# A two-block network on one core: convolution weights off GpSimd, a three-round inverse in the recurrence, finer modulation pieces

## The chip, the cores and the metric

The kernel runs on one core of a Trainium2 chip, as one program in one launch. The metric is the device time of an execution in microseconds (us), lower is better. The five engines are PE (matrix products), DVE (vector work, most of it elementwise), ACT (functions, copies and casts), POOL (GpSimd) and SP, which here only issues transfers (DMA).

## The reference, cut to what matters

Two blocks follow each other on 512 tokens of width 1024, in fp32. Each has two layers; each layer is a mixer and a feed-forward part, with a modulation (shift, scale, gate) computed from a condition vector by a matrix of its own. The parts that the change touches:

```python
# block 1, second mixer: a gated product, a depthwise convolution of width 31, norm, silu
def _conformer_conv(h, w_in, dw, dw_b, ln_g, ln_b, w_out):
    a, g = jnp.split(h @ w_in, 2, axis=-1)
    z = a * jax.nn.sigmoid(g)
    z = _depthwise_conv(z, dw, dw_b)
    z = jax.nn.silu(_layer_norm(z, ln_g, ln_b))
    return z @ w_out

# block 2, first mixer: a recurrence over time for 8 heads of 64, in both directions
def step(state, inp):
    r_t, w_t, k_t, v_t, kk_t, a_t = inp
    sa = jnp.einsum('bhvk,bhk->bhv', state, -kk_t)
    state = (state * w_t[:, :, None, :] + sa[..., None] * (kk_t * a_t)[:, :, None, :]
             + v_t[..., None] * k_t[:, :, None, :])
    return state, jnp.einsum('bhvk,bhk->bhv', state, r_t)

# ... with a bonus, added to the recurrence's normalised output
bonus = jnp.sum(f['r'][:, :, None] * f['k'] * prm['r_k'], axis=(2, 4))

# block 2, second mixer: one input projection for a neighbourhood and a global attention
p_ctx = u_ctx @ w_in
p_lat = u_lat @ w_in
```

The first mixer of block 2 joins the recurrence with a windowed attention; both run over 512 tokens and 256 context tokens.

## The kernel before, in words

**Products.** An fp32 product of the large weights runs as three products of rounded numbers (`mm3`, L300 to L304): high by high (L302), low by high (L303), high by low (L304). A weight comes by DMA on SP's queue (L285, `wraw_...`), ACT casts it to its high part (L289, `whi_...`), and an engine that is a parameter subtracts to get the low part (L290, `wlo_...`; DVE if nothing is said). L287 multiplies a down weight by a gate before that. hT, the layer's transposed input, is split in the same way (L277 high, L278 low).

**Stages, in us of the profiled execution.** Start 0 to 60; first mixer to 182; first feed-forward to 625; convolution mixer to about 900; second feed-forward to 1345; input products of the recurrence and of the windowed attention (`even`) to 1629; windowed attention, 24 units, to 1753; recurrence to 2117; output product and feed-forward to 2730; input products of the second layer (`odd`) to 2900; its attentions to 3055; the last output product and feed-forward to 3471.

**What sets the order.** A tile scheduler orders each engine's instructions from the code; some places are written out by hand. Modulations are computed in the gaps: `ada_store` puts 512 of a modulation's columns through `ada_part`: four loads of 512 KB (`adaw`, two buffers), 64 matmul records (`adaps`, L209), one ACT copy (`adarows`, L211), and stores. `todo` is a list of such pieces, and each call of `fill()` in a stage pops one.

**Convolution (`mixer1`).** 1024 channels are eight chunks. `gated(f)` makes the two products of a chunk (`cvps`), a sigmoid on ACT, and their gated product on DVE (L603, `hidl`). The 31 taps run as multiply-adds on DVE (L621) for chunks 0 to 4 and most of 7, and as three products with a diagonal matrix (`dg`, made by ACT) on PE for 12 taps of chunk 7 and all of 6 and 5 (`conv_pe`, `cvacc`); for these the chunk is split into zh and zl on DVE (L631, L632, L278) inside `conv_pe`. The projection's low weights wlo_cvin, and those of the first half of the output projection (wraw_dn, wlo_dn), are made on POOL. Behind the last tap PE transposes the chunks (`cvt`), DVE takes statistics (L675), and the result goes through a norm, silu and the output product.

**Even input (`even`).** A list of jobs is run `staggered`: K, Q, U are columns of the projection, W and C decays and rates, G gates, H the attention's heads, B the bonus products (`bops`, L1209) on inputs kd and plt of DVE.

**Recurrence.** Six steps of two chunks, in two directions d. For each, `operators` inverts a block-triangular matrix from the inverses Xd of its 16x16 diagonal blocks: in two doubling levels (16, then 32), V = MM[b] x XT (`pV`, copied by ACT to U), then X plus its product with U (`pX`, added by DVE, L1483), in both transposes at the first level. The result multiplies Aw (`pW`), and that QB (`pD`). In the trace the large buffers are called big, WhThi and WhTchi. The recurrence's first step (`PM`, on AB) begins behind four attention units; Xd comes from an earlier step through DRAM (L1451).

**Odd input (`odd`).** The values are products of six token tiles with four weight pieces (wraw_inv, whi_inv; `dps`), behind eight pieces of queries and keys whose results are stored and loaded again (okh, okl, oq on SP).

Of the kernel before, what the change touches and what calls it, by code (L numbers as in the profile page):

```python
# [21 lines left out]
KD = 8  # L22
# [35 lines left out]
def host_consts():  # L58
# [43 lines left out]
    for b in (16, 32):  # L102
        lv = (t // (2 * b) == u // (2 * b)) & (t % (2 * b) >= b) & (u % (2 * b) < b)
        c4.put(f"lv{b}", np.concatenate([lv & (p[:, None] // 64 == q) for q in range(2)], 1))
# [16 lines left out]
class Kernel:  # L121
# [77 lines left out]
    def ada_part(self, w, sil, c0, bufs=None):  # L199

        nc = self.nc
        acc = self.ps.tile([128, 512], F32, tag="tr", name="adaps", bufs=2)
# [253 lines left out]
    def ffn1(self, li, hT, done, gate, x):  # L456
# [7 lines left out]
        for gi, gn in enumerate(groups):  # L464
            src = []
            for _ in range(gn):
                o = []
                for f in (j, j + NH1):
                    w = self.w_up(wu, 128 * f, "up")
# [8 lines left out]
                self.fill()  # L478
# [10 lines left out]
    def mixer0(self, ws, hT, done, gate, x):  # L489
# [31 lines left out]
        for h in range(4):  # L521
            if h == 2:
                self.fill()
# [19 lines left out]
        for g, win in enumerate(WINDOWS):  # L543
            w = self.w_up(w_in, 1024 + 128 * g, "inz")
# [39 lines left out]
    def mixer1(self, hT, done, gate, x):  # L584
# [8 lines left out]
        def gated(f):  # L593
            self.fill()
# [32 lines left out]
        def conv_pe(f):  # L627
# [10 lines left out]
            nc.vector.tensor_tensor(wl, wf, wh.bitcast(F32), SUB)  # L638
            p = self.mmps("cvacc")
# [9 lines left out]
        order = (0, 1, 2, 3, 4, 7, 6, 5)  # L649
        for j, f in enumerate(order):  # L650
# [28 lines left out]
        conv_pe(5)  # L679
# [29 lines left out]
        with self.tc.issue_after(last.ins):  # L709
            self.down(w_out, src[:4], acc, True, gate=gate, x=x, eng=nc.gpsimd)  # L710
# [4 lines left out]
    def block1(self, xd):  # L715
# [35 lines left out]
        def ada(k, *qs):  # L751
            i, part = phases[k]
            return [lambda q=q: self.ada_store(ap[f"{part}_ada_w"][i], sil, 512 * q, ada1[k]) for q in qs]

        ada2 = [lambda j=j: self.ada_store(ap["w_ada_2"][j // 12], sil2, 512 * (j % 12), self.ada_d[j // 12])
                for j in range(24)]

        def columns():
# [7 lines left out]
                ada(1, 4, 5) + ["gate"] + ada(2, 0, 1, 2, 3) + ["mod"] + ada(2, 4, 5) + ada(3, 0, 1, 2, 3, 4, 5) + ada2[:6],  # L766
                ["gate"] + ["mod"] + ada2[6:12],
                ["gate"] + ada2[12:] + self.begin2()]
# [278 lines left out]
    def even(self, hT):  # L1047
# [200 lines left out]
        jobs += [W[0][3], H[2], B[2], C[0][3], H[3], W[1][3], C[1][3], H[4], H[5], B[3]]  # L1248
# [97 lines left out]
    def recurrence(self, st, R):  # L1346
# [107 lines left out]
        def operators(d, E):  # L1454


            Xd, Aw, QB, AD = (E[x] for x in ("Xd", "Aw", "QB", "AD"))
            X, XT = (v8(bufs[x][d]) for x in ("X", "XT"))
            for x, t in ((1, XT), (0, X)):
# [3 lines left out]
            MM = {}  # L1463
            for b, t in zip((16, 32), bufs["MM"][d]):
                MM[b] = v8(t)
                (nc.gpsimd if E["s"] else vec).tensor_tensor(t.rearrange("p (h q c) -> p h q c", h=8, q=2), E["M"][:, :, None, :].to_broadcast([128, 8, 2, 64]),
                                        c[f"lv{b}"].rearrange("p (q c) -> p q c", q=2)[:, None].to_broadcast([128, 8, 2, 64]), MUL)
# [8 lines left out]
            for b in (16, 32):  # L1476
# [83 lines left out]
        bufs = dict(Aw=at(10, 12, 2, 5), QB=at(11, 13, 7, 6), AD=at(16, 17, 18, 19, 4, 9, 22, 23), X=at(14, 0), XT=at(15, 1),  # L1560
# [378 lines left out]
```

## Time and profile before

| | |
|---|---|
| Median of 3 runs | 3477.03 us |
| All runs | 3480.14, 3477.03, 3469.45 us |
| Profiled execution: own time, span | 3472.81, 3471.0 us |
| Granted clock of PE, mean | 0.959 |
| Busy share: PE, DVE, ACT, POOL | 93%, 59%, 38%, 11% |

The page describes one execution. An engine's busy time is the time in which it works on something; the granted clock is the share of full speed (2.4 GHz, the other level being 1.2 GHz) that PE was given. In a row of the timeline the figure in brackets is the idle time before the instruction, and behind the arrow stands what ended it.

### The profile page before, as it was taken

How to read it: one execution, taken by the hardware profiler on the slowest of the kernel's cores; microseconds unless marked ns; L12 is line 12 of the kernel's file. 1: busy time of each engine (PE TensorE's matmuls, PEld its weight loads, DVE VectorE, ACT ScalarE, POOL GpSimd, SP SyncE). 2: the span in 40 equal slices, each digit the busy share in tenths (PEclk: the TensorE clock that was granted, in tenths of full speed). 3: DMA queues.
4: the chain of work that ended last, by engine and by line, in shares of the span. 5: the costliest groups of instructions: out<-in, count | busy, mean ns of one | idle time of the engine just before them, and what ended most of it. 6: DMA issues, size and time to landing. Idle time of an engine off the chain costs nothing. (4 is left out here: it accounts for less than half of the span.)

```text
span 3471.0 us, 50354 instructions
## 1 busy us (share of the span) xinstructions
PE 3216.5 (93%) x20031; PEld 2612.9 (75%) x20031; DVE 2053.2 (59%) x3772; ACT 1305.7 (38%) x2150; POOL 397.2 (11%) x218
## 2 busy tenths in 40 slices
PE   8989999868999998987898799999999998999998
PEld 5677777746776776875688798788888787878887
DVE  4675554897755567586767667533333735763445
ACT  3243332317423334443543334422222525753222
POOL 0020000540200000023033331010000200010001
PEclk9999999989999998998989899999999999999999
DMA  7645565440266432445322215672222365143332
GB/s 253 202 134 178 175 212 177 133 161 25 86 195 206 125 105 96 124 122 164 90 67 66 64 53 171 142 152 79 65 63 67 122 155 216 63 138 104 97 97 85
DMA packets 520693, 436.67 MB, mean 126 GB/s; under 512 B 91924, under 2 KB 450042, under 8 KB 518922
## 3 DMA queue, kind: packets, MB, share of 16 engines
q1 hardware_dynamic: 520458, 433.45, 41.4%
q8 instruction: 158, 2.59, 0.3%
q14 instruction: 77, 0.63, 0.1%
HBM read 368.96 MB, written 63.78 MB: 125 GB/s over the span
## 5 line engine op out<-in xcount | busy, mean ns | idle before, releaser
L302 PE MATMUL dnps<-whi_dn,hidh 128*128 128x512 f32 x1120 | 442.0, 395 | 3.5 <-ACT hidh L277 2.0
L303 PE MATMUL dnps<-wlo_dn,hidh 128*128 128x512 f32 x1120 | 438.9, 392 | 0.3
L304 PE MATMUL dnps<-whi_dn,hidl 128*128 128x512 f32 x1120 | 435.4, 391 | 1.2 <-DVE hidl L278 1.2
L290 DVE TENSOR_TENSOR wlo_dn<-wraw_dn,whi_dn 128x1024 fp32r<-128x1024 f32 x136 | 167.2, 1230 | 239.1 <-ACT whi_dn L289 238.3
L302 PE MATMUL upps<-hThi,whi_up 128*128 128x512 f32 (+1 forms) x768 | 295.7, 387 | 6.8 <-DVE hThi L277 6.7
L303 PE MATMUL upps<-hTlo,whi_up 128*128 128x512 f32 (+1 forms) x768 | 293.0, 383 | 4.8 <-DVE hTlo L278 4.8
L304 PE MATMUL upps<-hThi,wlo_up 128*128 128x512 f32 (+1 forms) x768 | 290.3, 379 | 0.0
L424 DVE TENSOR_TENSOR acc<-dnps,acc 128x512 f32<-128x512 f32 x200 | 136.7, 687 | 201.7 <-PE dnps L304 201.2
L302 PEld LDWEIGHTS dnps<-whi_dn,hidh 128*128 128x128 f32 x1120 | 210.2, 188 | 60.9 <-ACT hidh L277 7.0
L289 ACT CAST whi_dn<-wraw_dn 128x1024 fp32r<-128x1024 f32 x140 | 147.1, 1051 | 273.7 <-PE dnps L304 101.5
L303 PEld LDWEIGHTS dnps<-wlo_dn,hidh 128*128 128x128 f32 x1120 | 210.5, 188 | 47.1 <-issue 2.7
L304 PEld LDWEIGHTS dnps<-whi_dn,hidl 128*128 128x128 f32 x1120 | 209.8, 188 | 46.7 <-DVE hidl L278 3.4
L303 PE MATMUL up2ps<-hTlo,whi_ff 128*128 128x512 f32 (+1 forms) x576 | 214.5, 373 | 3.4 <-DVE hTlo L278 3.0
L302 PE MATMUL up2ps<-hThi,whi_ff 128*128 128x512 f32 (+1 forms) x576 | 212.7, 371 | 2.4 <-DVE hThi L277 2.4
L304 PE MATMUL up2ps<-hThi,wlo_ff 128*128 128x512 f32 (+1 forms) x576 | 212.1, 369 | 0.0
L290 DVE TENSOR_TENSOR wlo_up<-wraw_up,whi_up 128x1024 fp32r<-128x1024 f32 x88 | 111.1, 1262 | 135.5 <-ACT whi_up L289 134.6
L302 PEld LDWEIGHTS upps<-hThi,whi_up 128*128 128x128 f32 x768 | 147.2, 192 | 54.1 <-issue 12.4
L824 POOL TENSOR_TENSOR ag<-acc,gg 128x1024 f32<-128x1024 f32 x20 | 49.2, 2458 | 1124.8 <-DVE acc L424 1093.5
L303 PEld LDWEIGHTS upps<-hTlo,whi_up 128*128 128x128 f32 x768 | 147.5, 192 | 39.1 <-issue 9.9
L304 PEld LDWEIGHTS upps<-hThi,wlo_up 128*128 128x128 f32 x768 | 147.8, 193 | 26.1 <-issue 0.8
L289 ACT CAST whi_ff<-wraw_ff 128x1024 fp32r<-128x1024 f32 x64 | 67.2, 1052 | 245.9 <-PE dnps L304 202.3
L290 DVE TENSOR_TENSOR wlo_ff<-wraw_ff,whi_ff 128x1024 fp32r<-128x1024 f32 x64 | 80.8, 1264 | 126.7 <-ACT whi_ff L289 126.4
(528 smaller groups left out, 7431.0 us busy)
## 6 DMA issues: line engine op xcount, KB each, us to landing
adaw<-in_w_ada_dram SPq DMA_DIRECT2D x96, 512.0 KB
wraw_up<-in_ffn_w_up_dram SPq DMA_DIRECT2D x88, 512.0 KB
wraw_ff<-in_w_ff_dram SPq DMA_DIRECT2D x64, 512.0 KB
wraw_dn<-in_w_ff_dram SPq DMA_DIRECT2D x64, 512.0 KB
adaw<-in_ffn_ada_w_dram SPq DMA_DIRECT2D x48, 512.0 KB
wraw_dn<-in_ffn_w_down_dram SPq DMA_DIRECT2D x44, 512.0 KB
adaw<-in_mix_ada_w_dram SPq DMA_DIRECT2D x32, 512.0 KB
ab<-ab SPq DMA_DIRECT2D x32, 384.0 KB
```

The source lines that it names most:

```text
L289: nc.scalar.copy(hi, raw)
L290: (eng or nc.vector).tensor_tensor(lo, raw, hi, SUB)
L302: mm(out, a[0], b[0], start=first, stop=False)
L303: mm(out, a[0], b[1], start=False, stop=False)
L304: mm(out, a[1], b[0], start=False, stop=last)
L424: nc.vector.tensor_tensor(acc[:, t, c], p, acc[:, t, c], ADD)
L824: nc.gpsimd.tensor_tensor(ag, a, gg[:, 0 if t < NT else 1, :], MUL)
```

## The change

There are six edits. One: in the convolution the weights wlo_cvin, wraw_dn and wlo_dn are made by DVE, and a chunk for PE is split (`rounded`) as soon as it is gated. Two: `operators` forms one strictly lower block matrix MM (with all levels at once), NT = MM x XT, and three rounds of "NT x what is there, plus the first"; for direction 0 they run on Aw's product with XT, for direction 1 on XT itself, with `pW` behind. Three: the bonus product B[2] stands behind C[0][3] and H[3] in the list of jobs. Four: the recurrence begins behind eight attention units. Five: the odd values run over weight pieces outside and token tiles inside, three tiles at a time. Six: a modulation piece has 256 columns, issues both its loads first, and there are about twice as many calls of `fill()`.

```diff
     def ada_part(self, w, sil, c0, bufs=None):
...
         n = 512 if bufs else 256
-        for c in range(0, 512, n):
-            for h in range(0, KD, 4):
-                raw = bufs.pop(0) if bufs else self.adap.tile([128, 4, 256], F32, tag="adaw", name="adaw", bufs=self.nadaw)
-                nc.sync.dma_start(raw, w[128 * h:128 * h + 512, c0 + c:c0 + c + n].rearrange("(k p) c -> p k c", p=128))
-                for k in range(4):
-                    nc.tensor.matmul(acc[32 * k:32 * k + 32, c:c + n], sil[:, h + k, :], raw[:, k, :], start=h == 0, stop=h > 0)
-        rows = self.wp.tile([128, 512], F32, tag="adar", name="adarows", bufs=1)
+        acc = self.ps.tile([128, n], F32, tag="tr", name="adaps", bufs=2)
+        raw = []
+        for h in range(0, KD, 4):
+            raw.append(bufs.pop(0) if bufs else self.adap.tile([128, 4, 256], F32, tag="adaw", name="adaw", bufs=self.nadaw))
+            nc.sync.dma_start(raw[-1], w[128 * h:128 * h + 512, c0:c0 + n].rearrange("(k p) c -> p k c", p=128))
+        for h, r in zip(range(0, KD, 4), raw):
+            for k in range(4):
+                nc.tensor.matmul(acc[32 * k:32 * k + 32], sil[:, h + k, :], r[:, k, :], start=h == 0, stop=h > 0)
+        rows = self.wp.tile([128, n], F32, tag="adar", name="adarows", bufs=1)
...
     def ada_store(self, w, sil, c0, dst):
-        rows = self.ada_part(w, sil, c0)
-        for m in range(dst.shape[0]):
-            self.nc.sync.dma_start(dst[m, :, c0:c0 + 512], rows[m::32, :])
+        def piece(c):
+            rows = self.ada_part(w, sil, c)
+            for m in range(dst.shape[0]):
+                self.nc.sync.dma_start(dst[m, :, c:c + 256], rows[m::32, :])
+        return [partial(piece, c) for c in (c0, c0 + 256)]
...
         def gated(f):
-            self.fill()
             pp = []
             for ff in (f, f + KD):
-                w = self.w_up(w_in, 128 * ff, "cvin", nc.gpsimd)
+                self.fill()
+                w = self.w_up(w_in, 128 * ff, "cvin")
...
             gated(f)
+            if f in taps_pe:
+                parts.append((f, *rounded(f)))
             for _ in range(14 if j else 0):
                 next(taps)
             if j >= 6:
-                conv_pe(order[j - 1])
+                conv_pe(*parts.pop(0))
...
-            self.down(w_out, src[:4], acc, True, gate=gate, x=x, eng=nc.gpsimd)
+            self.down(w_out, src[:4], acc, True, gate=gate, x=x)
...
-        jobs += [W[0][3], H[2], B[2], C[0][3], H[3], W[1][3], C[1][3], H[4], H[5], B[3]]
+        jobs += [W[0][3], H[2], C[0][3], H[3], B[2], W[1][3], C[1][3], H[4], H[5], B[3]]
...
-            for b in (16, 32):
-                U = v8(R.tile([128, 1024], F32, tag=f"tD{d}", name="U", bufs=2))
+            NT = v8(R.tile([128, 1024], F32, tag=f"tD{d}", name="NT", bufs=2))
+            for hs in H4:
+                nc.scalar.copy(NT[:, hs], mm4("pV", *((XT, MM) if d else (MM, XT)), hs))
+            if not d:
                 for hs in H4:
-                    nc.scalar.copy(U[:, hs], mm4("pV", MM[b], XT, hs))
-                for tr in ((1, 0) if b == 16 else (1 - d,)):
-                    for hs in H4:
-                        t = (XT if tr else X)[:, hs]
-                        vec.tensor_tensor(t, mm4("pX", *((X, U) if tr else (U, X)), hs), t, ADD)
-            XT = X if d == 1 else XT
-            for hs in H4:
-                nc.scalar.copy(Aw[:, hs], mm4("pW", XT, Aw, hs))
+                    nc.scalar.copy(Y[:, hs], mm4("pW", XT, Aw, hs))
+            first, at, to = (Aw, Aw, Y) if d else (Y, Y, Aw)
+            for _ in range(3):
+                for hs in H4:
+                    vec.tensor_tensor(to[:, hs], mm4("pX", NT, at, hs), first[:, hs], ADD)
+                at = to
+            if d:
+                for hs in H4:
+                    nc.scalar.copy(Aw[:, hs], mm4("pW", X, at, hs))
...
-        for t in range(NT2):
-            p = mps()
-            for k in range(KD):
-                wt = ws[k // 2]
-                self.mm3(p, self.cols_of(hT, k, 128 * t, 128),
-                         (wt[0][:, k % 2, :], wt[1][:, k % 2, :]), k == 0, k == KD - 1)
-            nc.scalar.copy(cv[:, t, :], p)
+        for ts in (range(0, 3), range(3, NT2)):
+            ps = [mps() for t in ts]
+            for a, wt in zip(range(0, KD, 2), ws):
+                for t, p in zip(ts, ps):
+                    for k in (a, a + 1):
+                        self.mm3(p, self.cols_of(hT, k, 128 * t, 128),
+                                 (wt[0][:, k % 2, :], wt[1][:, k % 2, :]), k == 0, k == KD - 1)
+            for t, p in zip(ts, ps):
+                nc.scalar.copy(cv[:, t, :], p)
...
-                for _ in range(4):
+                for _ in range(8):
                     next(windowed)
```

On DVE in the convolution, before, at the splits of chunks 6 and 5: hidl_5062 is the gated product of chunk 5, hidl_5064 that of chunk 6, and the zl row is the split of chunk 6.

```order
L621 SCALAR_TENSOR_TENSOR hidh_5065<-hidl_5066,vec_e,hidh_5065 128x506
L287 TENSOR_TENSOR wraw_dn<-wraw_dn,gate 128x1024
L603 TENSOR_TENSOR hidl_5062<-cvps,sg 128x512
L631 MEMSET zh 128x15
L632 MEMSET zh 128x15
L631 MEMSET zl 128x15
L632 MEMSET zl 128x15
L278 TENSOR_TENSOR zl<-hidl_5064,zh 128x512
```

In the changed kernel, on DVE, from the gated product of chunk 6 (hidl_5174) on:

```order
L605 TENSOR_TENSOR hidl_5174<-cvps,sg 128x512
L633 MEMSET zh 128x15
L634 MEMSET zh 128x15
L633 MEMSET zl 128x15
L634 MEMSET zl 128x15
L623 SCALAR_TENSOR_TENSOR hidh_5167<-hidl_5168,vec_e,hidh_5167 128x511
L280 TENSOR_TENSOR zl<-hidl_5174,zh 128x512
L292 TENSOR_TENSOR wlo_cvin<-wraw_cvin,whi_cvin 128x1024 x2
L623 SCALAR_TENSOR_TENSOR hidh_5165<-hidl_5166,vec_e,hidh_5165 128x510
L623 SCALAR_TENSOR_TENSOR hidh_5167<-hidl_5168,vec_e,hidh_5167 128x510
```

The split of chunk 6 stood behind the gated product of chunk 5; now it stands six rows behind its own, and two wlo_cvin stand behind it. Chunk 7's split has moved in the same way.

On PE in the recurrence, before, the operators of the last step for one direction (a program's fp32 product is one of the counted rows here, and two records in a trace):

```order
L323 MATMUL pV<-big 128x128 x8
L323 MATMUL pX<-U,big 128x128 x8
L323 MATMUL pX<-big,U 128x128 x8
L323 MATMUL pV<-big 128x128 x8
L323 MATMUL pX<-big,U 128x128 x8
L323 MATMUL pW<-big 128x128 x8
L323 MATMUL pD<-big 128x128 x16
```

In the changed kernel, at the same place of PE, for one direction:

```order
L325 MATMUL pV<-big 128x128 x8
L325 MATMUL pX<-big,NT 128x128 x24
L325 MATMUL pW<-big 128x128 x8
L325 MATMUL pD<-big 128x128 x16
L325 MATMUL pz<-Z,big 64x64 x16
```

There is one group of V products in place of two, and the three groups of X products stand one behind the other.

## Rows read from the trace of the kernel before

**Rows 1.** Page, part 1: engine, busy us (share of the span), instructions.
```profile
PE 3216.5 (93%) x20031; PEld 2612.9 (75%) x20031; DVE 2053.2 (59%) x3772; ACT 1305.7 (38%) x2150; POOL 397.2 (11%) x218
```

**Rows 2.** Table by windows: us, busy us (instructions) per engine, PEclk, DMA share, GB/s.
```profile
625.00:700.00 75.00, 63.71 (x399) 52.05 (x398) 65.73 (x105) 27.20 (x37) 41.44 (x17) 0.89 0.46 141
700.00:776.00 76.00, 49.66 (x279) 33.62 (x278) 76.00 (x82) 12.40 (x16) 39.90 (x12) 0.85 0.50 161
776.00:860.00 84.00, 72.07 (x319) 56.86 (x319) 67.72 (x126) 60.96 (x161) 2.39 (x1) 0.95 0.08 26
...
1629.00:1753.00 124.00, 96.46 (x892) 75.42 (x891) 82.87 (x279) 68.11 (x212) 8.67 (x16) 0.90 0.39 111
1753.00:2117.00 364.00, 325.31 (x3947) 300.33 (x3946) 255.37 (x554) 130.73 (x239) 123.79 (x80) 0.91 0.25 71
```

**Rows 3.** Waits, 625 to 870 us: total us, times, longest.
```profile
PE cvacc L302 <- DVE zl L632: 22.8, 2, 19.0
...
PE adaps L209 <- DMA adaw<-in_w_ada_dram: 8.3, 4, 5.8
...
PE cvps L303 <- DVE hTlo L278: 7.3, 4, 3.9
```

**Rows 4.** Timeline of DVE, 770 to 870 us: start, us, instruction, idle before.
```profile
813.61 21.80 DVE L621 SCALAR_TENSOR_TENSOR hidh<-hidl,vec_e,hidh 128x497 f32<-128x497 f32 x28
848.77 0.43 DVE L675 BATCH_NORM_STATS2 cvst<-cvt 128x6 f32<-128x256 f32 x1 [13.36 <-PE cvt L667]
```

**Rows 5.** Groups by line, whole span: busy us, mean ns, idle before.
```profile
L621 DVE SCALAR_TENSOR_TENSOR hidh<-hidl,vec_e,hidh 128x503 f32<-128x503 f32 (+15 forms) x169 | 147.2, 916 | 1.9
...
L290 DVE TENSOR_TENSOR wlo_ine<-wraw_ine,whi_ine 128x1024 fp32r<-128x1024 f32 x21 | 25.6, 1218 | 14.7 <-ACT whi_ine L289 14.7
```

**Rows 6.** Groups by line on POOL, 670 to 836 us.
```profile
L290 POOL TENSOR_TENSOR wlo_cvin<-wraw_cvin,whi_cvin 128x1024 fp32r<-128x1024 f32 x9 | 25.3, 2815 | 31.9 <-ACT whi_cvin L289 28.7 <-PE adaps L209 3.1
```

**Rows 7.** Timeline of DVE, 636 to 655 us, the splits of hT.
```profile
640.90 2.50 DVE L278 TENSOR_TENSOR hTlo<-hTf,hThi 128x256 fp32r<-128x256 f32 x1
...
650.25 0.42 DVE L278 TENSOR_TENSOR hTlo<-hTf,hThi 128x256 fp32r<-128x256 f32 x1
```

**Rows 8.** Groups by line, recurrence, 1753 to 2117 us.
```profile
L323 PE MATMUL pV<-WhThi,WhTchi 128*128 128x128 f32 x192 | 28.7, 296 | 0.0
...
L323 PE MATMUL pV<-big 128*128 128x128 f32 x192 | 26.2, 292 | 0.2 <-DVE big L1483 0.2
...
L1483 DVE TENSOR_TENSOR big<-pX,big 128x512 f32<-128x512 f32 x36 | 24.7, 689 | 20.1 <-PE pX L323 19.9
```

**Rows 9.** Waits of PE, recurrence.
```profile
PE pW L323 <- DVE big L1483: 5.4, 1, 5.4
```

**Rows 10.** Timeline of PE, 1585 to 1595 us.
```profile
1589.11 2.90 PE L1209 MATMUL bops<-kd,consts 128*128 128x512 f32 x4 [11.41 <-DVE plt L1172]
...
1593.57 0.39 PE L303 MATMUL lowps<-spl,lwh 64*128 64x512 f32 x1
1593.80 0.39 PE L304 MATMUL lowps<-sph,lwl 64*128 64x512 f32 x1
```

**Rows 11.** Waits of PE, windowed attention, 1629 to 1753 us.
```profile
PE PM L323 <- DMA AB<-ab: 7.7, 1, 7.7
```

**Rows 12.** Timeline of SP's DMA issues, 1640 to 1790 us.
```profile
1709.10 2.62 SPq L1451 DMA_DIRECT2D Xd<-blkout  x4
```

**Rows 13.** Groups by line, whole span, the modulation matmuls.
```profile
L209 PE MATMUL adaps<-adaw,silc 128*32 128x256 f32 (+1 forms) x704 | 59.4, 427 | 12.6 <-DMA adaw<-in_mix_ada_w_dram 6.7 <-DMA adaw<-in_ffn_ada_w_dram 5.6
...
L209 PE MATMUL adaps<-adaw,sil 128*32 128x256 f32 x768 | 57.0, 393 | 16.2 <-DMA adaw<-in_w_ada_dram 15.3
```

**Rows 14.** Timeline of PE, 2855 to 2872 us.
```profile
2868.99 1.22 PE L302 MATMUL dps<-whi_inv,hThi 128*128 128x512 f32 x2 [8.01 <-ACT whi_inv L289]
```

**Rows 15.** Timeline of SP, 2800 to 2910 us.
```profile
2861.63 0.87 SPq L1032 DMA_DIRECT2D okl<-spl  x1
2862.55 1.88 SPq L285 DMA_DIRECT2D wraw_inv<-in_w_in_odd_dram  x2
```

More of the change, by code (lines that the diff above doesn't have):

```diff
@@ L101, in host_consts @@
     c4.put("dg", t // 16 == u // 16)
-    for b in (16, 32):
-        lv = (t // (2 * b) == u // (2 * b)) & (t % (2 * b) >= b) & (u % (2 * b) < b)
-        c4.put(f"lv{b}", np.concatenate([lv & (p[:, None] // 64 == q) for q in range(2)], 1))
+    c4.put("lo", np.concatenate([(t // 16 > u // 16) & (p[:, None] // 64 == q) for q in range(2)], 1))
     c4.put("dg2", p[:, None] // 16 == p[None] // 16)
@@ L201, in ada_part @@
         nc = self.nc
-        acc = self.ps.tile([128, 512], F32, tag="tr", name="adaps", bufs=2)
         n = 512 if bufs else 256
-        for c in range(0, 512, n):
-            for h in range(0, KD, 4):
-                raw = bufs.pop(0) if bufs else self.adap.tile([128, 4, 256], F32, tag="adaw", name="adaw", bufs=self.nadaw)
-                nc.sync.dma_start(raw, w[128 * h:128 * h + 512, c0 + c:c0 + c + n].rearrange("(k p) c -> p k c", p=128))
-                for k in range(4):
-                    nc.tensor.matmul(acc[32 * k:32 * k + 32, c:c + n], sil[:, h + k, :], raw[:, k, :], start=h == 0, stop=h > 0)
-        rows = self.wp.tile([128, 512], F32, tag="adar", name="adarows", bufs=1)
+        acc = self.ps.tile([128, n], F32, tag="tr", name="adaps", bufs=2)
[7 more added lines that the diff above has]
+        rows = self.wp.tile([128, n], F32, tag="adar", name="adarows", bufs=1)
         nc.scalar.copy(rows, acc)
@@ L521, in mixer0 @@
         for h in range(4):
-            if h == 2:
-                self.fill()
+            self.fill()
             w = self.w_up(w_in, 128 * h, "inu")
@@ L543, in mixer0 @@
         for g, win in enumerate(WINDOWS):
+            self.fill()
             w = self.w_up(w_in, 1024 + 128 * g, "inz")
@@ L593, in gated @@
         def gated(f):
-            self.fill()
             pp = []
             for ff in (f, f + KD):
-                w = self.w_up(w_in, 128 * ff, "cvin", nc.gpsimd)
+                self.fill()
+                w = self.w_up(w_in, 128 * ff, "cvin")
                 p = self.mmps("cvps")
@@ L625, in mixer1, with rounded @@
         taps_pe = {7: range(31 - 12, 31), 6: range(31), 5: range(31)}
-        def conv_pe(f):
+        def rounded(f):
             zh = self.tmp("zh", S + 2 * H, F32R)
@@ L638, in conv_pe @@
             nc.vector.tensor_tensor(wl, wf, wh.bitcast(F32), SUB)
+            return zh, zl, wh, wl
+        def conv_pe(f, zh, zl, wh, wl):
             p = self.mmps("cvacc")
@@ L649, in mixer1 @@
         order = (0, 1, 2, 3, 4, 7, 6, 5)
+        parts = []
         for j, f in enumerate(order):
             gated(f)
+            if f in taps_pe:
+                parts.append((f, *rounded(f)))
             for _ in range(14 if j else 0):
@@ L677, in stats @@
                 nc.scalar.copy(zt, p.rearrange("p (t f c) -> p t f c", t=2, f=2))
-        conv_pe(5)
+        conv_pe(*parts.pop(0))
         assert not self.todo
@@ L752, in ada @@
             i, part = phases[k]
-            return [lambda q=q: self.ada_store(ap[f"{part}_ada_w"][i], sil, 512 * q, ada1[k]) for q in qs]
-        ada2 = [lambda j=j: self.ada_store(ap["w_ada_2"][j // 12], sil2, 512 * (j % 12), self.ada_d[j // 12])
-                for j in range(24)]
+            return [f for q in qs for f in self.ada_store(ap[f"{part}_ada_w"][i], sil, 512 * q, ada1[k])]
+        ada2 = [f for j in range(24) for f in self.ada_store(ap["w_ada_2"][j // 12], sil2, 512 * (j % 12), self.ada_d[j // 12])]
         def columns():
@@ L765, in block1 @@
         todo = [ada(0,4,5)+[columns]+ada(1,0,1)+["gate"]+ada(1,2,3)+["mod"],
-                ada(1, 4, 5) + ["gate"] + ada(2, 0, 1, 2, 3) + ["mod"] + ada(2, 4, 5) + ada(3, 0, 1, 2, 3, 4, 5) + ada2[:6],
-                ["gate"] + ["mod"] + ada2[6:12],
-                ["gate"] + ada2[12:] + self.begin2()]
+                ada(1, 4, 5) + ["gate"] + ada(2, 0, 1, 2, 3) + ["mod"] + ada(2, 4, 5) + ada(3, 0, 1, 2, 3, 4, 5) + ada2[:12],
+                ["gate"] + ["mod"] + ada2[12:24],
+                ["gate"] + ada2[24:] + self.begin2()]
         for k, (i, part) in enumerate(phases):
@@ L1457, in operators @@
             Xd, Aw, QB, AD = (E[x] for x in ("Xd", "Aw", "QB", "AD"))
-            X, XT = (v8(bufs[x][d]) for x in ("X", "XT"))
-            for x, t in ((1, XT), (0, X)):
+            X, XT, Y = v8(bufs["X"]), v8(bufs["XT"][d]), v8(bufs["Y"][d])
+            for x, t in ((1, XT), (0, X))[:1 + d]:
                 nc.gpsimd.tensor_tensor(t.rearrange("p h (b s) -> p h b s", b=8),
@@ L1462, in operators @@
                                         c["dg2"].rearrange("p (b s) -> p b s", b=8)[:, None].to_broadcast([128, 8, 8, 16]), MUL)
[L1463 to L1467, printed above, removed]
+            t = bufs["MM"][d]
+            MM = v8(t)
+            (nc.gpsimd if E["s"] else vec).tensor_tensor(t.rearrange("p (h q c) -> p h q c", h=8, q=2), E["M"][:, :, None, :].to_broadcast([128, 8, 2, 64]),
+                                    c["lo"].rearrange("p (q c) -> p q c", q=2)[:, None].to_broadcast([128, 8, 2, 64]), MUL)
             H4 = [slice(0, 4), slice(4, 8)]
@@ L1559, in recurrence @@
         at = lambda *js: [W[j] for j in js]
-        bufs = dict(Aw=at(10, 12, 2, 5), QB=at(11, 13, 7, 6), AD=at(16, 17, 18, 19, 4, 9, 22, 23), X=at(14, 0), XT=at(15, 1),
-                    MM=[at(20, 21), at(3, 8)])
+        bufs = dict(Aw=at(10, 12, 2, 5), QB=at(11, 13, 7, 6), AD=at(16, 17, 18, 19, 4, 9, 22, 23), X=W[0], XT=at(15, 1), Y=at(14, 8), MM=at(20, 3))
         Z = []
```

1 line of the change is left out of this document (removed).

## The prediction

> **What bounds the kernel now.** I read the page's busy shares first, then the table by stages, then who is waited for inside the stages that the change touches, and last single rows there. The shares say that TensorE (PE) is the bound: busy 93% of the span, DVE 59%, ACT 38%, GpSimd (POOL) 11% [rows 1]. So time comes only from PE work removed, PE waits removed, or matmuls that run at the full granted clock in place of the half one. The stage table shows where this general rule fails [rows 2]: from 700 to 776 us PE is busy 49.66 of 76 us while DVE is busy 76.00 of 76, and the granted clock is 0.85. There the convolution is bound by DVE. From 1753 to 2117 us, the recurrence, PE is busy 325 of 364 us with DVE at 255: PE has the bound, DVE is close behind.
>
> The waits inside the convolution name one large one [rows 3]: PE stood 22.8 us for zl, 19.0 us of them at once. Beside it there are 8.3 us for modulation weights and 7.3 us for hTlo. The last statistic waits for PE's transposes 13.36 us and begins at 848.77 [rows 4]: at the stage's end PE itself is the last thing, with the products of chunks 6 and 5 one after the other.
>
> **The change, part by part.** The sum is made against the profiled execution, 3472.8 us (span 3471.0). That is 4.2 us below the median of the runs shown, 3477.0, so the forecast is read once against each.
>
> *Convolution.* The wait for zl is one of order. On DVE the split of chunk 6 stood behind the gated product of chunk 5 (the order rows of DVE show it), and that of chunk 7 behind the product of chunk 6; now each stands a few rows behind its own product. PE then has chunk 7's taps to run where it waited. Gain on PE: 22.8 us [rows 3], if DVE keeps up. DVE does: its 169 tap instructions took 916 ns in the mean [rows 5], but 21.80/28 = 779 ns where GpSimd is still [rows 4]. Without GpSimd's weight work they lose 169 x 0.137 = 23.2 us. Against this come the weight operations. Sixteen wlo_cvin go to DVE at 1.22 us, the mean of wlo_ine of the same shape there [rows 5]; nine of them lie between the first tap and the last [rows 6], 11.0 us, and seven ahead of the first, where DVE has slack (busy 65.7 of 75 us, [rows 2]). The eight weight operations of the output projection (four wraw_dn, four wlo_dn) cost up to 8 x 1.22 = 9.8 us; behind the last tap they lie in the statistics, in front of the down projection, where I charge 3 us for them. So DVE has 23.2 - 11.0 = 12 us less to do before the last tap, which ended at 813.61 + 21.80 = 835.4 and so comes to 823; four of the eight others ahead of it would make that 828. PE without its waits would end its chunk products at 848 - 22.8 = 825. The two agree to 3 us. hTlo: the split of 128x256 took 2.50 us beside a GpSimd operation and 0.42 alone [rows 7]; GpSimd's additions to x stay there and its five wlo_cvin go, so I take 3 of the 7.3 us. Both loads of a modulation piece are now issued ahead of its matmuls, a gain of about 1 of the 8.3 us. Convolution: -22.8 - 3 - 1 + 3 = -24. Bounds: -33 (all three waits of rows 3, 38.4, less 11.0 x 0.5) and -5 (DVE saturated, so that only 23.2 - 11.0 - 9.8 = 2.4 of its work and 3 of hTlo go).
>
> What takes the cover of GpSimd's slowness away is worth a sentence. Trainium skill, "SBUF — State Buffer", section "SBUF: two separate sides": the port pair that DVE and GpSimd share is an exclusive lock, and whoever starts first holds it for the whole instruction. The trace agrees for hTlo: its 2.50 us hold 2.1 us of standing still.
>
> *Recurrence.* Before, a direction inverts its triangular matrix in two doubling levels (V, then X, twice); now one product NT and three rounds of "NT times what is there, plus the first". The number of X products (288 of the program's matmuls) and of W products (96) stays, the V products fall from 192 to 96. The two V rows of the trace hold 192 records each, 28.7 and 26.2 us busy [rows 8]; a program matmul of this kind has two records. Half of 54.9 us is 27.4 us of PE. ACT loses 24 of its 48 copies and GpSimd 16 expansions; both wait for PE and for buffers more than PE for them, so they count nothing. What is late next: each of the 36 additions on DVE (L1483, 689 ns [rows 8]) now has the next round of X waiting behind it, with only the other half's four matmuls, about 1.0 us, as cover. Before, PE waited 5.4 us once for such an addition [rows 9]; I give back one more of that size: -27.4 + 5.4 = -22. Bounds: -34 (the clock of 0.91 [rows 2] means 18% of 364 us, 66 us, at half speed; a fifth of the 33 us lost there besides) and 0 (every saved matmul turned into a wait).
>
> *Bonus product one step later.* PE waited 11.41 us at 1589 for plt and kd on DVE [rows 10]. In front of the product now stand the 48 matmuls of a column piece of H[3], 24 of 512 columns at 0.23 us from start to start [rows 10] and 24 of 256 at half of that, 8.3 us, and six lowps of the same widths, 1.0 us: 9.3 us of cover. I take -9.5, with the one ropeps matmul; bounds -11.4 and -4 (DVE reaches kd later because H[3]'s evictions now stand in its way).
>
> *Recurrence behind eight units.* PM waits 7.7 us for AB at 1649 [rows 11]; four more attention units, (1753 - 1629)/24 = 5.2 us each, are over 20 us of cover. The transfers behind them have slack: Xd is issued at 1709 [rows 12] and the products that use it begin behind 1753, so 20 us of delay are hidden. -8; bounds -12 (clock 0.90 in that stage [rows 2]) and 0.
>
> *Modulations in halves.* The same matmuls, in twice as many slots with half the length each; 48 ACT copies of adarows become 92, shorter ones; 68 stores on SP become 136. PE's waits ahead of them are 12.6 and 16.2 us over the span [rows 13], nearly all for loads, 8.3 of them in the convolution, counted above: 20.5 are open. Some stand at the program's start, where the code stays; smaller pieces spread the other loads, and I take -6. Bounds -20.5, and +12: in mixer0 two loads now stand on SP ahead of the first weight piece, and a store costs up to 0.87 us of SP's time (an okl store, [rows 15]), 68 x 0.87 = 59 us in a queue that is issued well ahead, of which I let a fifth show.
>
> *Odd values by weight piece.* PE waits 8.01 us at 2868.99 for whi_inv [rows 14]. The loads of pieces 1 and 2 are issued at 2862.55, right behind the last okl store [rows 15], and SP's order there does not change; PE before already takes piece 0 of four tiles first. So this edit does not do what its name says: 0, bounds -3 and +2.
>
> **Sum.** -24 - 22 - 9.5 - 8 - 6 - 0 = -70: 3472.8 - 70 = 3403 for a profiled execution, 3407 on the median of runs.
>
> **The rivals.** *DVE takes the convolution's gain.* Its row of 76.00 in 76 us [rows 2] speaks for it: 24 more weight operations at 1.22 us are 29 us, more than the 23.2 us that the taps lose. Against it: seven of the 24 lie ahead of the taps and some behind them. Time: 3407 + 24 = 3431. The Trainium skill, "Perfetto Trace Analysis", section "Optimizing Scalar/DVE Operations", says that work of a saturated DVE may be worth moving to ScalarE or even GpSimd, and adds that between DVE and GpSimd it might not help because of the shared port. Its first half is this rival, its second half the forecast.
>
> *The recurrence gives its matmuls back as waits.* For it: the chain X, addition, X has one more link of DVE in a row. Against it: before, the chain of a direction had five such boundaries too, at 5.4 us in the worst. Time: 3407 + 22 = 3429. With the first rival at once: 3453.
>
> *The other side: the chain of X and additions becomes the bound.* There are 36 boundaries at which an addition must be through DVE, busy 255 of 364 us [rows 2]. If its queue delays each by over 70/36 = 1.9 us, the whole gain is lost; at 2.6 us the time is 3407 + 94 = 3501. The worst seen was 5.4 us, once [rows 9], and that is also the largest sum of any line there that waits for an addition of L1483, which speaks against it.
>
> *The clock comes back.* Granted 0.89, 0.85 and 0.95 in the convolution [rows 2]: at half speed that is 16.5 + 22.8 + 8.4 = 47.7 us, 24 us to win where the waits that precede a fall of the clock go. With half of that, and as much in the recurrence: 3407 - 24 = 3383.
>
> **How the numbers follow.** Forecast 0.60, clock 0.10, DVE in the convolution 0.12, recurrence given back 0.11, both 0.04, chain 0.03. The spread of the runs is 0.3%, 10 us, and that is what can be told from no change. All cases but the chain lie over 10 us below 3477; of the last 0.03 and of the case with both I put 0.03 at "within" and 0.03 at "slower", faster has 0.94. Range: 3380 (clock) to 3440 (one rival, and a little), 0.85 by these cases.
>
> **What would show it.** In the convolution: no PE wait on zl over 5 us, taps at 0.78 us, first statistic before 830, DVE still near 100% from 700 on. In the recurrence: half the V records, waits of PE on L1483's additions under 15 us together. No wait of bops over 2 us, none of PM; the wait of 8 us on whi_inv stays. I am wrong if the taps stay at 0.9 us without GpSimd, if PE waits for wlo_cvin on DVE, or if the stage of the recurrence is not at least 12 us shorter.

## The result, and the profile after

The changed kernel takes 3420.1 us in the median (3416.3 to 3428.4, 4 runs) against 3475.0 for the kernel before: ratio 0.985, 95% interval 0.982 to 0.987. Timed once more beside the last experiments it had 3417.8 us, ratio 0.983 (0.981 to 0.985). Forecast was 3407, with a range of 3380 to 3440. So it is faster by some 55 to 60 us where 70 were forecast. The profiled execution has a span of 3416.9 us. Part 1 of its page, which answers to [rows 1]:

```profile
PE 3191.8 (93%) x19839; PEld 2593.8 (76%) x19839; DVE 2036.0 (60%) x3794; ACT 1289.4 (38%) x2170; POOL 295.8 (9%) x178
```

PE's share has not moved: PE has 25 us less to do, GpSimd 101 us less, and the rest of the gain is PE's waiting. The table by windows shows the convolution, from its first matmul to its last, and the recurrence, from its first to the next stage's (columns as in [rows 2]):

```profile
636.20:843.60 207.40, 183.07 (x997) 141.16 (x998) 190.10 (x336) 102.81 (x229) 11.70 (x4) 0.92 0.38 118
1708.40:2061.00 352.60, 312.11 (x3747) 283.38 (x3747) 250.94 (x551) 116.66 (x215) 86.48 (x63) 0.88 0.26 73
```

For the kernel before the same stretches are 235.7 and 363.9 us long. In the convolution GpSimd was busy 74.19 us before and is busy 11.70 us now, and DVE, with more instructions (336 for 315), is busy 17 us less. From 700 to 776 us, where [rows 2] has PE busy 49.66 us and DVE 76.00, PE is now the full engine:

```profile
700.00:776.00 76.00, 75.64 (x391) 56.28 (x390) 71.30 (x118) 29.98 (x73) 0.00 (x0) 1.00 0.46 143
```

The groups by line from 640 to 836 us say why; they answer to [rows 5]:

```profile
L623 DVE SCALAR_TENSOR_TENSOR hidh<-hidl,vec_e,hidh 128x500 f32<-128x500 f32 (+15 forms) x169 | 117.2, 738 | 1.4
L292 DVE TENSOR_TENSOR wlo_cvin<-wraw_cvin,whi_cvin 128x1024 fp32r<-128x1024 f32 x13 | 15.7, 1220 | 3.0 <-ACT whi_cvin L291 2.9
```

The 169 taps take 738 ns each in place of 916, 30 us in all. Taken one by one, the taps of the kernel before show where these 30 us were: 130 of them meet no operation of GpSimd and take 737 ns in the mean, none over 754; 39 meet one and take 1515, the longest 2909. PE's waits from 625 to 845 us (total, times, longest), which answer to [rows 3], no longer have zl among them; two waits in the statistics, for ACT, are what is late next:

```profile
PE cvb L711 <- ACT acc L705: 8.9, 1, 8.9
PE cvt L675 <- ACT acc L685: 7.4, 3, 4.8
...
PE adaps L209 <- DMA adaw<-in_w_ada_dram: 1.7, 5, 0.6
```

In the recurrence the groups by line, which answer to [rows 8], show half the V records, and the X products under their new names:

```profile
L325 PE MATMUL pX<-big,NT 128*128 128x128 f32 x432 | 64.5, 308 | 8.7 <-DVE big L1493 8.5
...
L325 PE MATMUL pX<-WhThi,NT 128*128 128x128 f32 x144 | 20.5, 298 | 0.0
...
L325 PE MATMUL pV<-WhThi,WhTchi 128*128 128x128 f32 x96 | 16.5, 319 | 0.0
...
L325 PE MATMUL pV<-big 128*128 128x128 f32 x96 | 13.5, 296 | 0.0
```

From 1317 to 1592 us the wait of the bonus product is down from 11.41 us [rows 10] to this:

```profile
PE bops L1216 <- DVE kd L1209: 1.5, 1, 1.5
```

And on PE's timeline the odd values wait as before, to be read against [rows 14]:

```profile
2812.48 1.22 PE L304 MATMUL dps<-whi_inv,hThi 128*128 128x512 f32 x2 [8.49 <-ACT whi_inv L291]
```

The wait for whi_inv is 8.49 us where it was 8.01.

### The profile page after: what moved, and what is told of

It reads as the page before. It is cut to its first block, busy times and chain, and to the rows that moved or that the text cites. A ratio compares the mean times of both kernels' runs of the same rounds, so it can differ in the third digit from the quotient of the medians.

```text
span 3416.9 us, 50115 instructions
## 1 busy us (share of the span) xinstructions
PE 3191.8 (93%) x19839; PEld 2593.8 (76%) x19839; DVE 2036.0 (60%) x3794; ACT 1289.4 (38%) x2170; POOL 295.8 (9%) x178
## 5 line engine op out<-in xcount | busy, mean ns | idle before, releaser
L306 PEld LDWEIGHTS dnps<-whi_dn,hidl 128*128 128x128 f32 x1120 | 209.9, 188 | 47.0 <-DVE hidl L280 3.9
L306 PEld LDWEIGHTS upps<-hThi,wlo_up 128*128 128x128 f32 x768 | 146.8, 192 | 28.2 <-issue 2.1
L291 ACT CAST whi_up<-wraw_up 128x1024 fp32r<-128x1024 f32 x88 | 92.2, 1048 | 175.4 <-PE upps L305 59.8
```

Source lines behind the costliest of these rows:

```text
L291: nc.scalar.copy(hi, raw)
L306: mm(out, a[1], b[0], start=False, stop=last)
```

## The experiments

Every kernel was timed beside the kernel before, in 3 to 5 rounds. The stage lengths below are read from each run's trace: convolution from the first cvps to the last cvb, input products from the first up2ps to the first sc, windowed attention from there to the first tok, recurrence from there to the last py, odd from the first product with whi_ino to the last dps. The expectation of e7 speaks of 131 us for the odd stage; cut in this way it has 166. A length comes from one profile of each run and carries the scatter of a single execution.

| | ratio to before (95%) | convolution | input products | attention | recurrence | odd |
|---|---|---|---|---|---|---|
| before | 1 | 235.6 | 280.2 | 123.8 | 364.3 | 167.6 |
| changed | 0.985 (0.982 to 0.987) | 207.4 | 273.9 | 116.3 | 353.0 | 166.1 |
| e1 | 0.998 (0.997 to 0.999) | 233.9 | 280.2 | 121.4 | 370.3 | 167.7 |
| e2 | 0.990 (0.988 to 0.991) | 206.1 | 279.4 | 120.7 | 361.1 | 167.6 |
| e3 | 0.996 (0.994 to 0.998) | 237.1 | 282.3 | 120.4 | 348.8 | 166.8 |
| e4 | 0.988 (0.987 to 0.990) | 206.9 | 273.8 | 118.5 | 366.1 | 168.4 |
| e5 | 1.000 (0.998 to 1.002) | 239.6 | 279.5 | 124.3 | 367.8 | 166.5 |
| e6 | 0.996 (0.994 to 0.997) | 233.7 | 272.4 | 118.8 | 368.2 | 167.9 |
| e7 | 0.983 (0.981 to 0.985) | 206.8 | 272.6 | 117.9 | 345.5 | 163.5 |
| e8 | 0.987 (0.985 to 0.989) | 217.9 | 273.0 | 121.5 | 346.8 | 169.3 |
| e9 | 0.983 (0.981 to 0.985) | 207.0 | 273.2 | 115.6 | 345.8 | 169.8 |
| e10 | 0.984 (0.982 to 0.986) | 209.9 | 272.5 | 117.2 | 351.2 | 164.9 |
| e11 | 0.979 (0.978 to 0.980) | 208.0 | 260.9 | 118.7 | 346.9 | 164.0 |
| e12 | 0.977 (0.976 to 0.979) | 207.0 | 257.3 | 118.6 | 342.8 | 162.5 |

**e1, the early split alone.** To the kernel before:

```diff
+            if f in taps_pe:
+                parts.append((f, *rounded(f)))
...
-                conv_pe(order[j - 1])
+                conv_pe(*parts.pop(0))
```

> The kernel before, with one part of the convolution edit alone: a chunk for PE is split as soon as it is gated; the weights stay on GpSimd. If the order of the splits is what cost PE its 22.8 us, the wait for zl goes and the convolution stage (235.7 us before, from the first input product to the last transpose back, 207.4 us after) is 20 us or more shorter, the time about 3455. If DVE, slowed by GpSimd, sets the end, the wait only moves: the taps stay at 0.9 us, the last tap stays within 5 us of its place (835 us), and the stage wins 13 us at most (PE's 13.4 us between the last tap and the first statistic), time 3462 or more.

Measured: 3467.9 us, 7.6 us below the kernel before; the stage of its profile is 1.7 us shorter, and where the rest lies is not shown. The tap row of its groups by line, its longest wait of PE from 625 to 870 us, and the place on ACT's timeline just before the end of that wait:

```profile
L621 DVE SCALAR_TENSOR_TENSOR hidh<-hidl,vec_e,hidh 128x503 f32<-128x503 f32 (+15 forms) x169 | 149.4, 927 | 1.9
```

```profile
PE cvacc L302 <- ACT dg L646: 12.4, 2, 11.3
```

```profile
778.88 0.62 ACT L277 CAST zh<-hidl 128x512 fp32r<-128x512 f32 x1 [13.82 <-DVE zh L631]
```

The wait for zl is down to 0.5 us and most of it stands under other names: 12.4 us for dg, 3.0 for zh. The dg that PE waits for are made by ACT right behind this zh, and ACT itself had stood 13.82 us for DVE. The taps still take 927 ns, and the row of 28 taps ends at 838.8 us for 835.4 before. The order was a symptom; what set the end was DVE.

**e2, the weights on DVE alone.**

```diff
-                w = self.w_up(w_in, 128 * ff, "cvin", nc.gpsimd)
+                w = self.w_up(w_in, 128 * ff, "cvin")
...
-            self.down(w_out, src[:4], acc, True, gate=gate, x=x, eng=nc.gpsimd)
+            self.down(w_out, src[:4], acc, True, gate=gate, x=x)
```

> The kernel before, with the other part alone: wlo_cvin, wraw_dn and wlo_dn of the convolution on DVE, the splits in their old order. If GpSimd's hold on DVE is the cost, the taps fall from 916 to about 740 ns, 30 us over 169 taps, against some 20 us of weight work that DVE takes over: the stage is 8 to 15 us shorter and PE still waits for zl, time about 3463. If instead the saturated DVE pays for the added work, the stage is as long as before or longer, time 3475 or more.

Measured: 3442.0 us, the stage 29.5 us shorter: the whole of the changed kernel's gain there, with the splits in their old order. The tap row of its groups by line:

```profile
L621 DVE SCALAR_TENSOR_TENSOR hidh<-hidl,vec_e,hidh 128x508 f32<-128x508 f32 (+15 forms) x169 | 117.0, 738 | 1.4
```

Both expectations fell short, the first by half (8 to 15 us), the second altogether: DVE's busy time in the stage fell from 207 to 190 us although it makes the weights as well. The wait for zl, 22.8 us before, is 0.3 us in this run: as soon as DVE is faster, its queue ahead of zl is shorter too.

**e8, GpSimd beside the taps.** To the changed kernel; nothing uses the result:

```diff
+                x = self.tmp("extra")
+                for q in range(0, KD, 4):
+                    h = w[0].bitcast(F32)[:, q:q + 4, :]
+                    nc.gpsimd.tensor_tensor(x.rearrange("p (k c) -> p k c", k=4), h, h, SUB)
```

> The changed kernel; behind each projection weight of the convolution GpSimd does two subtractions of 128x512 whose result nothing uses. DVE's own instructions are the same, so this measures GpSimd's hold alone. If GpSimd's operations stretch the taps, those that meet one take 1.5 to 3 us in place of 0.74, the mean of the taps rises to 0.83 us or more and the stage (207 us) by 10 to 20 us: 3430 to 3440. If the added weight work and the order were what counted, and the lock is no matter, the stage stays within 3 us and the time is 3420.

Measured: 3435.8 us, the stage 10.5 us longer. The rows of the taps, of GpSimd's extra work and of wlo_cvin on DVE from 636 to 870 us:

```profile
L627 DVE SCALAR_TENSOR_TENSOR hidh<-hidl,vec_e,hidh 128x500 f32<-128x500 f32 (+15 forms) x169 | 125.0, 782 | 1.4
...
L603 POOL TENSOR_TENSOR extra<-whi_cvin 128x512 f32<-128x512 f32 x30 | 51.0, 1723 | 61.2 <-ACT whi_cvin L291 48.7 <-DVE hidl L609 12.4
...
L292 DVE TENSOR_TENSOR wlo_cvin<-wraw_cvin,whi_cvin 128x1024 fp32r<-128x1024 f32 x15 | 23.5, 1576 | 4.5 <-ACT whi_cvin L291 4.5
```

With DVE's own work the same, the taps take 782 ns for 738 (under the 830 expected) and wlo_cvin 1576 for 1220. GpSimd's work by itself stretches DVE, and the stage with it. One by one: 31 taps meet an operation of GpSimd, and 10 of these take over 1 us, up to 1.52; the other 138 take 735 ns. A tap is stretched by up to 0.78 us here and by up to 2.17 us in the kernel before, where GpSimd's operations were twice as long. The run gives back 10.5 of the 28.2 us, with GpSimd busy 60.5 us in the stage for 74.2 before and with the splits early; how the other 18 us divide is not shown.

**e3 and e4, the inverse alone, and everything but the inverse.** e3 takes the diff of `operators` into the kernel before, e4 takes it out of the changed one.

> The kernel before, with the nested inverse alone; the recurrence still begins behind four attention units. In the changed kernel the stage was 11.3 us shorter (363.9 to 352.6) where 22 had been forecast, with PE 13.1 us less busy and 82 us at half clock against 68. Theory clock: the matmuls are gone, but PE's waits lie otherwise and the clock is granted less, so here too the stage is 9 to 14 us shorter, its half-clock time 78 us or more, and its work counted at full clock 18 to 22 us less. Theory start: the later start behind eight units costs it; then the stage is 20 us or more shorter here, half-clock time near 68. Theory chain: the additions on DVE set the pace; then the waits of PE for them rise by 8 us or more. Time 3465 by the first and third, 3454 by the second.

> The changed kernel with the doubling inverse of before put back, all other edits in. Theory clock: about 11 us more than the changed kernel, 3431; the recurrence stage is 362 to 366 us with about 68 us at half clock. Theory start: the old inverse also pays for the later start, the stage is 372 us or more, time 3440. The convolution stage should stay near 207 us, and the modulation and odd stages as in the changed kernel.

Measured: e3 3459.8 us, stage 348.8; e4 3436.9, stage 366.1. The window of the recurrence in e4, in e3, and in e9, the changed kernel profiled again:

```profile
1709.80:2075.90 366.10, 329.28 (x3949) 303.42 (x3949) 254.61 (x553) 131.08 (x239) 124.09 (x80) 0.90 0.25 70
```

```profile
1750.00:2098.80 348.80, 307.22 (x3750) 279.50 (x3750) 251.04 (x552) 116.88 (x214) 86.93 (x64) 0.90 0.26 74
```

```profile
1709.20:2055.00 345.80, 305.22 (x3750) 277.59 (x3750) 250.41 (x551) 116.90 (x214) 86.86 (x64) 0.91 0.27 74
```

> The changed kernel once more, beside the next two and for its recurrence stage: with the new inverse the stage was 353.0, 348.8, 345.5 and 346.8 us in four profiles, with the old one 364.3, 370.3, 361.1, 366.1, 367.8 and 368.2. Expected 345 to 354 and 3420.

The theory of the clock falls: the changed kernel's first profile, at a granted clock of 0.88, was an exception. In e9 the same code got 0.91, and the stage took 345.8 us; the other profiles of the new inverse have 0.90 to 0.92, those of the old one 0.89 to 0.91. With the old inverse six profiles of the stage have 361.1 to 370.3 us, mean 366.3; with the new one eight have 342.8 to 353.0, mean 347.6. The edit is worth 18.7 us, not the 11.3 that the first pair of profiles shows. The theory of the late start falls as well (e3, with the early start, is not shorter than the others), and that of the chain: PE's waits for L1493's additions in the changed kernel are

```profile
PE pX L325 <- DVE big L1493: 8.5, 9, 3.9
```

and 0.8 us at pD, 9.3 in all. The old inverse lost 8.9 us: 5.4 [rows 9], 3.1 and 0.2 twice.

**e5, the modulation in halves alone** (its hunks from `ada_part` to `todo`, and the calls of `fill()`).

> The kernel before, with the modulation edit alone (pieces of 256 columns, both loads first, more calls of fill). By the forecast's term it is 6 us shorter, 3469. By the stages of the changed kernel it gives nothing: the first mixer starts its first product 3 us later, the two feed-forwards win 3 us together; then 3474 and within 0.2% of before. In its convolution the wait for modulation loads (8.3 us) should fall to about 2, and nothing come of it while DVE sets the pace there.

Measured: 3476.9 us, ratio 1.000 (0.998 to 1.002). The term of 6 us is not there; up to some 5 us can't be told. In its convolution PE waits 4.7 us for modulation loads (8.3 before, about 2 expected) and 30.1 us for zl (22.8 before): nothing came of the shorter wait, as the second expectation had it.

**e6, the bonus product and the eight units alone** (two lines of the diff).

> The kernel before, with the bonus product one step later and the recurrence behind eight units. The changed kernel's stages say 6.3 us for the input products (280.2 to 273.9) and 7.5 for the windowed attention (123.8 to 116.3): 3461. The forecast's two terms were 9.5 and 8: 3457. If a wait takes their place (a first order of ropeps or of the attention's DVE work), each stage wins under 3 us: 3470 or more.

Measured: 3466.3 us. The input products are 7.8 us shorter, the attention 5.0. Over all profiles: 273.1 against 280.3 us, and 118.1 against 122.1, so 7.2 and 4.0. The attention's two groups overlap (115.6 to 121.5 with eight units, 120.4 to 124.3 with four), so its 4.0 is rough. PM still waits for AB, 3.4 us.

**e7, the value pieces' loads between the key pieces.** To the changed kernel:

```diff
+        def keys_up(i):
+            ps = ups(512 + 128 * i, NT2)()
+            ws.extend(self.w_down(w_in, 256 * j, 1024, "inv") for j in range(len(ws), i))
+            return ps
...
-                       + [(ups(512 + 128 * i, NT2), partial(ck, i)) for i in range(4)])
-        ws = [self.w_down(w_in, 256 * i, 1024, "inv") for i in range(4)]
+                       + [(partial(keys_up, i), partial(ck, i)) for i in range(4)])
+        ws += [self.w_down(w_in, 256 * i, 1024, "inv") for i in range(len(ws), 4)]
```

> The changed kernel; the loads of the four value pieces are issued between the key pieces, ahead of the key stores on SP. PE still waits 8.5 us for whi_inv in the changed kernel, so the edit by weight piece won nothing. If SP's order is the cause, that wait goes and the odd stage (131 us) is about 8 us shorter: 3412. If the buffers of raw weights are the cause, the key weights come late in its place and the time stays at 3420.

Measured: 3418.7 us; the stage has 163.5 us, where the changed kernel's two profiles have 166.1 and 169.8. Its longest wait of PE from 2640 to 2850 us:

```profile
PE up2ps L304 <- ACT whi_ino L291: 6.4, 1, 6.4
```

The wait for whi_inv is gone, and a key piece's whi_ino is late by 6.4 us in its place: the second expectation held, but not in full. With the first value piece one key piece later (e10 to e12) the waits for whi_inv are 2.8 to 4.1 us, and none is for whi_ino. In these four runs the stage takes 162.5 to 164.9 us, in the ten others 166.1 to 169.8: the earlier loads win 4 us in the mean, half of the wait.

**e10 and e11, a lean version, and GpSimd off the input products.** e10 is the kernel before with e2, e3, e6, the odd values by weight piece and earlier loads of the value pieces. e11 changes three more lines:

```diff
-            nc.gpsimd.tensor_tensor(t, rows[:, 2, i % 2], inc, MUL)
+            nc.vector.tensor_tensor(t, rows[:, 2, i % 2], inc, MUL)
...
-            nc.gpsimd.tensor_tensor(t, t, einv, MUL)
+            nc.vector.tensor_tensor(t, t, einv, MUL)
...
-                nc.gpsimd.tensor_tensor(kd, kd, part[i, 1], ADD)
+                nc.vector.tensor_tensor(kd, kd, part[i, 1], ADD)
```

> What the runs bear out, without the rest: the convolution's weights on DVE, the nested inverse, the later bonus product, eight units, and the value pieces' loads between the key pieces (the first ahead of the last key weight, so that no key weight waits); no early split and no finer modulation pieces. If the two parts left out are worth nothing, as runs e1 to e5 say, and the odd wait of 8 us goes, it is at 3412, below the changed kernel by 5 to 10 us. If early split and halves matter once DVE is relieved, it is at 3425 or more.

> The same, and in the input products of the recurrence GpSimd's 20 operations on ab and kd go to DVE too. There GpSimd stretches DVE by about 27 us (of 34 in that stage), but PE has the bound. If relieving DVE pays wherever GpSimd works, the stage (273 us) is 10 us shorter or more; if only where DVE sets the pace, it stays within 4 us.

Measured: e10 3423.3 us, no better than the changed kernel (the second feed-forward is 7 us longer than there; e5 alone did not show that halves are worth it, and these two runs don't settle it). Over all profiles the second feed-forward takes 473.6 us with halves and 477.3 without, and the convolution begins at 639.5 us and at 637.3: 1.5 us together, which the scatter covers. e11 3406.0 us, the stage 11.6 us shorter than in e10, so the expectation that it stays was wrong. The windows of the stage in e10 and in e11:

```profile
1332.70:1605.20 272.50, 248.26 (x1393) 208.85 (x1392) 203.05 (x315) 119.60 (x187) 60.43 (x38) 0.93 0.43 125
```

```profile
1325.10:1586.00 260.90, 245.39 (x1393) 208.26 (x1393) 183.19 (x333) 118.41 (x187) 16.02 (x18) 0.93 0.46 131
```

DVE has 18 instructions more and is busy 20 us less. PE runs the same 1393 matmul records; of the 11.6 us, 2.9 are of its busy time and 8.7 of its waiting, at short waits for DVE and ACT that lie all over the stage. Whether PE gains by DVE's relief or because the 20 results themselves come earlier is not shown.

**e12, the changed kernel with both additions.**

> The changed kernel with the two additions that won: ab and kd of the recurrence's input products on DVE instead of GpSimd (20 operations), and the value pieces' loads between the key pieces. Run e11 against e10 says 11.6 us for the first in its stage (272.5 to 260.9), e7 against the changed kernel 1 to 4 us for the second: 3404 against 3419, stage 259 to 264 us. If e11's gain needed the parts that e10 left out, the stage stays at 273 and the time at 3417.

Measured: 3398.4 us, ratio 0.977 (0.976 to 0.979), below both kernels; the stage has 257.3 us (259 to 264 expected).

## Why the prediction was right, and where its steps were not

**The convolution: the size was right (24 forecast, 28.2 measured), the cause was not.** The step "the wait for zl is one of order" fell: the early split alone takes 1.7 us off the stage (e1), the weights on DVE alone 29.5 us (e2). The same prediction had the right term beside it: GpSimd stretches the taps, 23.2 us by [rows 4, 5], 30.0 measured. It then treated DVE's relief as what makes the wait's removal possible, while the wait was only where DVE's lateness showed. The row of DVE in [rows 2], busy 76.00 of 76 us, said that already: a wait of PE for an operation that stands behind others on a full DVE is a wait for DVE's whole queue. e8 shows the hold itself.

The term for the taps was too small because it set two different measures against each other: 916 ns is the mean duration of a tap, 21.80/28 = 779 ns the distance between starts. By duration a tap that GpSimd leaves alone takes 737 ns, and 169 x 0.179 us is 30 us. That the sum came out within 4 us was in part luck: the modulations' wait fell by 6.6 us where 1 was charged, hTlo's by 4.9 where 3 was, and the waits for ACT in the statistics (cvb and cvt in the rows above) rose by 9.0 where 3 was. Nor was 835.4 us the end of the taps: two more stood behind the first statistic, to 850.8. The signs held: the last tap of the changed kernel ends at 820.4 us (823 forecast) and its first statistic begins at 810.5 (before 830).

**The rival that the clock comes back** had little of it. Over the stage the granted clock rose from 0.88 to 0.92, but PE's busy time fell by 3.6 us only; the other 24.7 were idle time.

**The rival that a saturated DVE takes the gain back** fell: 24 more operations cost it 29 us by the sum, and GpSimd's absence returned more than that. The Trainium skill, "Perfetto Trace Analysis", section "Optimizing Scalar/DVE Operations", warns that moving work between DVE and GpSimd might not help, as they share a port of SBUF; for the weights on GpSimd this was the sentence to weigh, and e2 agrees with it (235.6 us with them there, 206.1 without). The rule behind it, in the Trainium skill, "SBUF — State Buffer", section "SBUF: two separate sides", is that of a GpSimd operation and a DVE operation with two inputs in SBUF, as the taps have, whichever starts first holds the shared pair of ports for its whole instruction while the other stands still. The taps agree with it: in the kernel before they take 737 ns alone and up to 2909 beside GpSimd, in e8 735 and up to 1521.

**The recurrence: 22 forecast, 18.7 over fourteen profiles.** The mechanism held: half the V records are gone, and PE's waits for the additions are 9.3 us for 8.9, where 5.4 more were charged. What was too large is the term of the V products: they gave 54.9 - 30.0 = 24.9 us for the 27.4 charged, as the 192 records that stay are busy 156 ns each where all 384 had 143, and the X products took more: 64.5 + 20.5 = 85.0 us busy against 82.9 in the two first profiles. In e9 PE's busy time in the stage is 20.0 us lower than before and its idle time 1.9 us higher. One sign of being wrong, a stage not at least 12 us shorter, stood in the first pair of profiles (11.3 us); the fourteen take it back. That the chain of additions becomes the bound did not come about. (For direction 1 the three rounds run on Aw itself and not on XT, as the diff shows; the product with X stands behind them.)

**The bonus product: 9.5 forecast, 7.2 measured.** Its wait fell to 1.5 us; what is late next is ropeps, 3.6 us for ACT's row. **Eight units: 8 forecast, 4.0 measured.** Twenty us of cover did not hide AB: with eight units and the old inverse PM still waits 3.3 us (e4) and 3.4 (e6), where it waits 4.5 to 7.7 with four. In the changed kernel that wait is gone, but an attention product waits 6.3 us for bos (0.9 before). This comes with the new inverse and not with the eight units: in e3, with four units, PM does not wait and bos costs 8.1 us; in e4 and e6 it costs 1.1 and 0.9. Why the inverse moves the wait is not shown.

**Modulations: 6 forecast, 0 within 5 us measured** (e5). **Odd values: 0 forecast and found**, for the reason given: the loads stand behind the key stores on SP. e7 adds that this is only half of it: with two buffers of raw weights, an earlier load of a value piece went with a later key piece, and 4 of the 8 us were won.

The sum by the stages is -28.2 - 18.7 - 7.2 - 4.0 - 0 = -58, and the two timings say -55 and -60. The forecast's excess of 12 us over that is the modulations' 6, the units' 4 and small parts of the others, less the convolution's 4.

## What to carry to other kernels

Where an engine is full in a stretch, a wait for it is not removed by putting one operation earlier; look for what makes the engine slow there, and compare the mean of a repeated instruction with its time where the neighbour is still, by durations on both sides. Work on GpSimd beside DVE is not free: count what it adds to DVE's instructions before counting what it takes off them, also in stages where PE looks like the bound (e11). Before a stage's length is explained from two profiles, look at its length in profiles of kernels that leave it alone.

## What the hardware showed that was not expected

The same code in the recurrence took 361 to 370 us in six profiles (old inverse) and 343 to 353 in eight (new one); the granted clock over the stage was 0.88 in the changed kernel's first profile and 0.91 in its second, with PE's idle time the same within 0.1 us (352.60 - 312.11 and 345.80 - 305.22). The hold works in both directions. The shortest of e8's extra subtractions took 1.03 us on GpSimd, by its span in the profile; this one took eight times as long:

```profile
695.61 8.19 POOL L603 TENSOR_TENSOR extra<-whi_cvin 128x512 f32<-128x512 f32 x1 [6.59 <-ACT whi_cvin L291]
```

Beside it DVE ran ten taps one behind the other, from 695.13 to 701.76 us and none over 0.74, and a wlo_cvin in its usual 1.21. The subtraction ended 1.0 us after DVE had begun the gated product (702.83), whose inputs are cvps and sg. So it is not always GpSimd that wins: of the 31 taps of e8 that meet one of its operations, 21 stay under 1 us.
